# Token sums of a Strassen FFN made between the rows of the output projection, and two whole gate columns per FFN where there were four

## The chip, the cores and the metric

One core of one Trainium2 chip runs the whole kernel as one program. The metric is the device time of that program in microseconds, the median of several executions; lower is better. The core has five engines that each run their own stream of instructions in order: PE (TensorE, matmuls), DVE (VectorE), ACT (ScalarE), POOL (GpSimd) and SP (SyncE). SP and POOL issue the DMAs here. They wait for each other through semaphores.

## The reference

A two-layer decoder trunk over 512 tokens of width 1024, all in float32. Layer 0 mixes with a gated DeltaNet, layer 1 with sliding-window attention; both attend to 256 memory tokens as well. Each layer then adds the mixed heads through `w_out`, and a SwiGLU FFN of width 2816:

```python
x = x + jnp.concatenate([mix_out.astype(x.dtype), mem_o.astype(x.dtype)], axis=-1) @ w_out[layer]
x = x + swiglu(rms_norm(x, ln_ffn[layer]), w_gate_up[layer], w_down[layer])
...
def swiglu(h, w_gate_up, w_down):
    gu = h @ w_gate_up
    return (jax.nn.silu(gu[..., :D_FF]) * gu[..., D_FF:]) @ w_down
```

The change touches the first line's product and sum, and the product `h @ w_gate_up` of the second.

## The kernel before

**Layout.** Everything is kept with features on the 128 partitions and the 512 tokens along the free axis. The residual stream is eight tiles `x0` to `x7` (trace name `x`, 128 x 512), one for each block of 128 features.

**Exact products.** Float32 accuracy comes from splitting every operand into a high part and a remainder: ACT copies the high part (`whi` of a weight, `h` of an activation, line 148), DVE subtracts it from the original (`wlo` at L171, `l` at L171 or L174). A product of one 128 x 128 weight block is then three matmuls (`mm3`, L154): `whi` with `h`, `whi` with `l`, `wlo` with `h`. A *row* or *column* of 128 output features needs eight blocks, 24 matmuls of 512 tokens. A weight tile is loaded by SP into one of two `wraw` buffers (L197), split into one of three `whi`/`wlo` buffers, and its `wraw` buffer is free for the next load only when DVE has made `wlo`.

**Output rows.** `output` (both layers) makes eight rows of the output projection, row `m` for `x[m]`, `m` from 0 to 7. The three first rows are begun ahead, in pieces between the last steps of the mixer (`rest`), and end together; the others follow one by one. After a row DVE adds it into `x[m]`, ACT and DVE make the FFN's activation `h`, `l` from `x[m]` and its gain (`split_gain`), and the squares are added up (`sq`, `sqa`) for the norm. The norm's factor `rstd` is multiplied in after the FFN's products.

**Columns of the FFN.** The FFN has 22 gate and 22 up columns. Most are made two at a time by `quarters`, a Strassen-Winograd scheme: the two columns' weights and the tokens are cut in halves, and seven products with half the features and half the tokens take the place of eight. Each product is 12 matmuls of 256 tokens into a bank `g`, and needs one 512-wide weight tile (`wraw`, or a sum of two weight blocks `ws`, which SP loads and POOL adds to with an accumulating DMA) split by ACT and DVE. It also needs sums over the two halves of the tokens: `token_sums(j)` makes four of them from `x[j]` and `x[j+4]`: one small product (`fs`), four quarter-size instructions (`fu`), two copies on ACT and two subtractions on DVE into `T` tiles. All four sets, j = 0 to 3, must exist before the first product `t1`.

**What fills the time until then.** In the first half of each FFN (`f0 == 0`) gate columns 0 to 3 are made whole, 24 matmuls of 512 tokens each into banks `pj`; the norm's two matmuls stand inside column 1. The token sums are written behind columns 0 and 1 (j = 0, 1) and behind columns 2 and 3 (j = 2, 3). Then come the up columns 0 and 1 by quarters, and so on; ten pairs in this half.

**What sets the order.** Each engine runs its stream in order. The streams are put together by the framework's scheduler from the program order and a model of its own, so an instruction may stand earlier or later in its engine's stream than it was written. A tile pool's memory is given to a later pool when its scope has closed, and the first writer of the new tile waits for the last reader of the old.

## Time and profile before

| | |
|---|---|
| median of 3 executions | 1141.31 us (1141.19 to 1141.54) |
| the profiled execution | 1140.89 us |
| its span | 1139.0 us |
| mean granted TensorE clock | 0.998 |

The span is the time from the first to the last instruction of the trace; the execution's own time is 1.9 us longer. All stamps below are microseconds from the start of the span. The stages that matter here: layer 0's output rows run from about 255 to 305, its gate columns 0 to 3 until 327.8, the quarters until 427; layer 1's rows end at about 788.6, its gate columns at 810.9, its quarters at 910. In a row of a timeline stand start, length, engine, line, operation, output <- input, shape, count, and in brackets the engine's idle time before it and what ended that.

### The profile page before, as it was taken

How to read it: one execution, taken by the hardware profiler on the slowest of the kernel's cores; microseconds unless marked ns; L12 is line 12 of the kernel's file. 1: busy time of each engine (PE TensorE's matmuls, PEld its weight loads, DVE VectorE, ACT ScalarE, POOL GpSimd, SP SyncE). 2: the span in 40 equal slices, each digit the busy share in tenths (PEclk: the TensorE clock that was granted, in tenths of full speed). 3: DMA queues.
4: the chain of work that ended last, by engine and by line, in shares of the span. 5: the costliest groups of instructions: out<-in, count | busy, mean ns of one | idle time of the engine just before them, and what ended most of it. 6: DMA issues, size and time to landing. Idle time of an engine off the chain costs nothing.

```text
span 1139.0 us, 19670 instructions
## 1 busy us (share of the span) xinstructions
PE 1121.6 (98%) x7476; PEld 992.7 (87%) x7476; DVE 841.6 (74%) x1592; ACT 632.1 (55%) x1274; POOL 86.2 (8%) x97
## 2 busy tenths in 40 slices
PE   7999999999999999999999999999999999999996
PEld 6888887887899998899998888888999988999986
DVE  6754887776889987389876868959799743899754
ACT  7569572365566653256653656855566522566533
POOL 0120000000101100011100000010011100111000
PEclk9999999999999999999999999999999999999999
DMA  8434342324667744567723421153477733677232
GB/s 311 128 114 113 120 107 98 95 91 148 188 145 188 186 129 126 159 146 188 185 72 93 134 74 57 43 133 122 126 183 179 199 98 106 150 185 185 70 99 91
DMA packets 73971, 152.76 MB, mean 134 GB/s; under 512 B 17756, under 2 KB 18420, under 8 KB 73876
## 3 DMA queue, kind: packets, MB, share of 16 engines
q1 hardware_dynamic: 62356, 130.52, 37.4%
q0 software_dynamic: 11520, 20.98, 11.7%
q8 instruction: 59, 0.97, 0.4%
q14 instruction: 36, 0.29, 0.1%
HBM read 144.51 MB, written 6.96 MB: 133 GB/s over the span
## 4 chain that ended last, share of the span: by engine, by line
PE 95%; DVE 2%; ACT 1%; DMA 1%; issue 0%; SPq 0%; DVEq 0%; ACTq 0%
PE pj L154 47%; PE g L154 37%; PE sc L154 6%; PE pt L154 2%; PE qk L154 2%; PE pt L168 1%; PE g L168 1%; DMA wraw<-in_wmk 1%; DVE wlo L171 1%; ACT whi L148 0%; ACT sm L142 0%; SPq L329 0%; DVE x L171 0%; DVE l L174 0%; DVE stats L836 0%
## 5 line engine op out<-in xcount | busy, mean ns | idle before, releaser
L148 ACT ACTIVATE whi<-wraw 128x512 fp32r<-128x512 f32 (+2 forms) x331 | 244.1, 746 | 241.9 <-PE pj L154 151.2
L171 DVE TENSOR_TENSOR wlo<-wraw,whi 128x512 fp32r<-128x512 f32 (+2 forms) x331 | 273.0, 835 | 105.8 <-ACT whi L148 99.8
L154 PE MATMUL pj<-h,whi 128*128 128x512 f32 (+1 forms) x676 | 265.4, 393 | 0.1
L154 PE MATMUL pj<-l,whi 128*128 128x512 f32 (+1 forms) x676 | 263.7, 390 | 0.0
L154 PE MATMUL pj<-h,wlo 128*128 128x512 f32 (+1 forms) x676 | 263.4, 390 | 0.0
L154 PE MATMUL g<-T,whi 128*128 128x256 f32 x1280 | 228.1, 278 | 0.2
L154 PEld LDWEIGHTS g<-T,whi 128*128 128x128 f32 x1280 | 194.7, 188 | 1.8 <-DVE fu L174 1.8
L154 PE MATMUL g<-T,wlo 128*128 128x256 f32 x640 | 177.8, 278 | 0.0
L154 PEld LDWEIGHTS pj<-h,whi 128*128 128x128 f32 x676 | 126.9, 188 | 28.4 <-issue 3.5
L154 PEld LDWEIGHTS pj<-h,wlo 128*128 128x128 f32 x676 | 127.0, 188 | 25.8 <-DVE wlo L171 0.4
L154 PEld LDWEIGHTS pj<-l,whi 128*128 128x128 f32 x676 | 127.1, 188 | 24.7 <-DVE l L171 0.4
L154 PE MATMUL g<-h,whi 128*128 128x256 f32 (+1 forms) x492 | 138.4, 281 | 0.0
L154 PE MATMUL g<-h,wlo 128*128 128x256 f32 (+1 forms) x492 | 138.0, 280 | 0.0
L154 PE MATMUL g<-l,whi 128*128 128x256 f32 (+1 forms) x492 | 138.0, 280 | 0.0
L154 PEld LDWEIGHTS g<-T,wlo 128*128 128x128 f32 x640 | 120.1, 188 | 0.0
L154 PEld LDWEIGHTS g<-l,whi 128*128 128x128 f32 x492 | 92.3, 188 | 0.8 <-issue 0.2
L154 PEld LDWEIGHTS g<-h,whi 128*128 128x128 f32 x492 | 92.3, 188 | 0.8 <-issue 0.2
L154 PEld LDWEIGHTS g<-h,wlo 128*128 128x128 f32 x492 | 92.3, 188 | 0.5
L1104 POOL DMA_DIRECT2D ws<-in_wgu x40 | 35.3, 882 | 705.7 <-ACT sq L151 237.7
L148 ACT ACTIVATE whi<-ws 128x512 fp32r<-128x512 f32 x80 | 50.4, 631 | 49.3 <-PE g L154 40.2
L171 DVE TENSOR_TENSOR fu<-pj,rstd 128x512 f32<-128x512 f32 (+1 forms) x34 | 22.4, 660 | 54.3 <-PE pj L154 54.2
L171 DVE TENSOR_TENSOR wlo<-ws,whi 128x512 fp32r<-128x512 f32 x80 | 54.9, 686 | 6.4 <-ACT whi L148 6.3
(384 smaller groups left out, 1649.4 us busy)
## 6 DMA issues: line engine op xcount, KB each, us to landing
wraw<-in_wgu SPq DMA_DIRECT2D x48, 512.0 KB, 4.3
ws<-in_wgu SPq DMA_DIRECT2D x80, 256.0 KB, 3.6
ws<-in_wgu POOLq DMA_DIRECT2D x80, 256.0 KB, 4.9
wraw<-in_wdn SPq DMA_DIRECT2D x48, 384.0 KB, 3.2
wraw<-in_win SPq DMA_DIRECT2D x26, 512.0 KB, 3.6
wraw<-in_wgu SPq DMA_DIRECT2D x40, 256.0 KB, 4.7
wraw<-in_wout SPq DMA_DIRECT2D x16, 512.0 KB, 3.6
wraw<-in_wdn SPq DMA_DIRECT2D x16, 256.0 KB, 2.7
```

What stands on the lines that cost most here:

```text
L148: self.copied = self.nc.scalar.activation(out, in_, AF.Copy, **kw).ins
L154: return self.chained(self.nc.tensor.matmul(out, lhsT, rhs, start=start, stop=stop, skip_group_check=more).ins)
L168: return self.chained(self.nc.tensor.transpose(out, in_, self.ident[:k, :k]).ins)
L171: return eng.tensor_tensor(out=out, in0=a, in1=b, op=op).ins
L1104: nc.gpsimd.dma_start(s1, a22, accum_op=ALU.add)
```

## The change

It does three things.

1. The rows of the output projection are made in the order of `TURN`, 0 4 1 5 2 6 3 7. A row's place in the order is now called `r`; the bank goes by `r`, the weights, the gain and the `x` tile by `TURN[r]`. The gate columns take the blocks of `h` in the same order.
2. After every second row but the last, `output` makes the token sum of the two tiles just finished: j = 0, 1 and 2. The helper tiles come from the `sq` buffers (the small product) and a new pool `turn` (`raw`, two tiles); the six `T` tiles come from a new pool `tok` that stays open to the end. The fourth sum, j = 3, is made in the FFN.
3. Only gate columns 0 and 1 are whole. Gate columns 2 and 3 are made by `quarters` like the others.

At the end of the program the six `T` buffers of `tok` and the two of the FFN's pool serve where eight of the FFN's pool did.

```diff
+TURN = (0, 4, 1, 5, 2, 6, 3, 7)
...
+                    self.tok = pool("tok")
...
-        def part(m, *ks):
-            if m not in rows:
-                rows[m] = self.weight(self.a["wout"][layer, m]), self.row_bank(m), []
-            w, ps, done = rows[m]
+        def part(r, *ks):
+            if r not in rows:
+                rows[r] = self.weight(self.a["wout"][layer, TURN[r]]), self.row_bank(r), []
+            w, ps, done = rows[r]
...
+        def work():
+            return self.t(xp, [P, T], F32, "sq", 2)[:, :T // 2], [self.t(tp, [P, T], F32, "raw", 2) for _ in range(2)]
+
+        def row(r, *ks):
+            ps = part(r, *ks)
             if ps is None:
                 return
+            m = TURN[r]
             self.tt(nc.vector, self.x[m], ps, self.x[m], ALU.add)
-            hl = self.pair(hpool)
-            self.split_gain(self.x[m], self.gain(G_FFN[layer], m), *hl)
-            h.append(hl)
+            h[m] = self.pair(hpool)
+            self.split_gain(self.x[m], self.gain(G_FFN[layer], m), *h[m])
             self.acc = self.accumulate(xp, self.acc, self.x[m])
+            if r % 2 and r < KD - 1:
+                sums.append(self.token_sums(layer, r // 2, h, work, self.tok, 6))
...
-            return self.project(col(f, 0), h, "pj", between=between)
+            return self.project(col(f, 0), h, "pj", TURN, between=between)
+
+        def work():
+            return self.t(fp, [P, T // 2], F32, "fs", 3), [self.t(fp, [P, T], F32, "fu", 3) for _ in range(2)]
...
                 two = [gate(0), gate(1, {1: [norm]})]
                 whole += [gated(ps) for ps in two]
-                sums += [self.token_sums(fp, layer, f, h) for f in range(2)]
-                for f in (2, 3):
-                    whole.append(gated(gate(f)))
-                    sums.append(self.token_sums(fp, layer, f, h))
+                sums.append(self.token_sums(layer, 3, h, work, fp, 2))
```

**Layer 1, DVE, from the end of the first three rows.** Before, with the tile's own number in its name (`x0_` is tile x0, `wlo_1342` the fifth row's weight remainder, `wlo_1349` the sixth's):

```order
L171 TENSOR_TENSOR x0_546_2807<-pj_1282_7762,x0_546_2807 128x512
L171 TENSOR_TENSOR x1_547_2808<-pj_1301_7871,x1_547_2808 128x512
L171 TENSOR_TENSOR wlo_1335_8058<-wraw_1333_8055,whi_1334_8057 128x1024
L174 SCALAR_TENSOR_TENSOR l_1325_8028<-x0_546_2807,gains_2_67,h_1324_8027 128x512
L171 TENSOR_TENSOR x2_548_2809<-qk_1313_7935,x2_548_2809 128x512
L174 SCALAR_TENSOR_TENSOR l_1328_8038<-x1_547_2808,gains_2_67,h_1327_8037 128x512
L171 TENSOR_TENSOR sqa_1326_8031<-sqa_1326_8031,sq_1329_8041 128x512
L174 SCALAR_TENSOR_TENSOR l_1331_8049<-x2_548_2809,gains_2_67,h_1330_8048 128x512
L171 TENSOR_TENSOR sqa_1326_8031<-sqa_1326_8031,sq_1332_8052 128x512
L171 TENSOR_TENSOR wlo_1342_8097<-wraw_1340_8094,whi_1341_8096 128x1024
```

The same place after the change begins in the same way, with x0, x4, the fourth row's remainder, an `l`, x1 and an `l`. From there on (`wlo_1354` is the fifth row's remainder):

```order
L172 TENSOR_TENSOR sqa_1328_8102<-sqa_1328_8102,sq_1331_8112 128x512
L179 TENSOR_SCALAR sq_1332_8116<-x0_546_2807,gains_2_67 128x256
L175 SCALAR_TENSOR_TENSOR l_1338_8135<-x1_547_2808,gains_2_67,h_1337_8134 128x512
L175 SCALAR_TENSOR_TENSOR raw_1333_8117<-x0_546_2807,gains_2_67,sq_1332_8116 128x256
L175 SCALAR_TENSOR_TENSOR raw_1334_8118<-x4_550_2811,gains_2_67,sq_1332_8116 128x256
L175 SCALAR_TENSOR_TENSOR raw_1333_8117<-x4_550_2811,eps_5_71,raw_1333_8117 128x256
L172 TENSOR_TENSOR sqa_1328_8102<-sqa_1328_8102,sq_1339_8138 128x512
L175 SCALAR_TENSOR_TENSOR raw_1334_8118<-x4_550_2811,eps_5_71,raw_1333_8117 128x256
L172 TENSOR_TENSOR T_1336_8125<-raw_1333_8117,T_1335_8124 128x512
L172 TENSOR_TENSOR x5_551_2812<-pj_1343_8147,x5_551_2812 128x512
L172 TENSOR_TENSOR T_1336_8125<-raw_1334_8118,T_1335_8124 128x512
L172 TENSOR_TENSOR wlo_1354_8197<-wraw_1352_8194,whi_1353_8196 128x1024
```

The whole token sum of x0 and x4, and the add of the fourth row into x5, now stand ahead of the fifth row's remainder.

**Layer 0, DVE, the same place.** After the change x0, the fourth row's remainder, x1, an `l`, the fifth row's remainder, x4, the small product, an `l` and an `sqa` come first; then (`wlo_592` is the sixth row's remainder):

```order
L175 SCALAR_TENSOR_TENSOR raw_564_2873<-x0_546_2807,gains_2_67,sq_563_2872 128x256
L175 SCALAR_TENSOR_TENSOR raw_565_2874<-x4_550_2811,gains_2_67,sq_563_2872 128x256
L175 SCALAR_TENSOR_TENSOR raw_564_2873<-x4_550_2811,eps_5_71,raw_564_2873 128x256
L175 SCALAR_TENSOR_TENSOR l_569_2891<-x1_547_2808,gains_2_67,h_568_2890 128x512
L175 SCALAR_TENSOR_TENSOR raw_565_2874<-x4_550_2811,eps_5_71,raw_564_2873 128x256
L172 TENSOR_TENSOR T_567_2881<-raw_564_2873,T_566_2880 128x512
L172 TENSOR_TENSOR sqa_559_2858<-sqa_559_2858,sq_570_2894 128x512
L172 TENSOR_TENSOR x5_551_2812<-pj_574_2903,x5_551_2812 128x512
L172 TENSOR_TENSOR T_567_2881<-raw_565_2874,T_566_2880 128x512
L172 TENSOR_TENSOR wlo_592_2992<-wraw_590_2989,whi_591_2991 128x1024
```

Before, the sixth row's remainder stood directly behind the add of the fourth row, and the fifth row's remainder directly ahead of that add; no part of a token sum stood among the rows of layer 0 until the seventh was done.

**Layer 0, SP, the first loads of the FFN.** Before (1024-wide `wraw` are the whole gate columns 0, 1, 2 and 3; `ws_647` and `ws_648` are the first pair's weight sums):

```order
L197 DMA wraw_603_3083<-in_wgu 128x1024
L197 DMA wraw_607_3114<-in_wgu 128x1024
L197 DMA wraw_624_3186<-in_wgu 128x1024
L1102 DMA ws_647_3286<-in_wgu 128x512
L197 DMA wraw_634_3234<-in_wgu 128x1024
L1103 DMA ws_648_3287<-in_wgu 128x512
L1107 DMA wraw_649_3292<-in_wgu 128x512
```

After (gate columns 0 and 1, then the first pair's and the second pair's own columns, `wraw_636` and `wraw_654`, then the first pair's sums):

```order
L198 DMA wraw_618_3133<-in_wgu 128x1024
L198 DMA wraw_622_3164<-in_wgu 128x1024
L198 DMA wraw_636_3223<-in_wgu 128x1024
L198 DMA wraw_654_3341<-in_wgu 128x1024
L1110 DMA ws_637_3225<-in_wgu 128x512
L1111 DMA ws_638_3226<-in_wgu 128x512
L1115 DMA wraw_639_3231<-in_wgu 128x512
```

The first sum's load moved behind a fourth 1024-wide load, which waits for the remainder of gate column 1. In layer 1 the loads of the first two pairs' sums, issued between 738.8 and 754.8 before, moved behind the load of the first pair's own column, which waits for the remainder of gate column 0.

More of the change, by code (lines that the diff above doesn't have):

```diff
@@ L282, in rest @@
                                 row(m, k)
-                    h = self.output(xp, 0, part, self.bpool, rest)
+                    h, sums = self.output(xp, 0, part, self.bpool, rest)
             with opened("ffn0", side="right") as fp, self.banks(pj=2, g=6):
-                self.ffn(fp, xp, 0, h, self.apool, rope=True)
+                self.ffn(fp, xp, 0, h, sums, self.apool, rope=True)
             with self.banks(pj=2, qk=1, pt=4):
@@ L289, in build @@
                     mix, rest = self.swa(sp, xp)
-                    h = self.output(xp, 1, self.opened_rows(1, mix), self.apool, rest)
+                    h, sums = self.output(xp, 1, self.opened_rows(1, mix), self.apool, rest)
             with opened("ffn1", side="right") as fp, self.banks(pj=2, g=6):
-                self.ffn(fp, xp, 1, h, self.bpool)
+                self.ffn(fp, xp, 1, h, sums, self.bpool)
     def load_constants(self, cp):
@@ L903, in attend, with row_bank @@
         return steps
-    def row_bank(self, m):
-        if m % 3 < 2:
+    def row_bank(self, r):
+        if r % 3 < 2:
             return self.bank("pj")
@@ L932, in output, with ffn @@
         self.weng = nc.vector
-        h = []
+        h, sums = {}, []
         self.acc = None
-        def row(m, *ks):
-            ps = part(m, *ks)
+        def work():
+            return self.t(xp, [P, T], F32, "sq", 2)[:, :T // 2], [self.t(tp, [P, T], F32, "raw", 2) for _ in range(2)]
+        def row(r, *ks):
+            ps = part(r, *ks)
             if ps is None:
                 return
+            m = TURN[r]
             self.tt(nc.vector, self.x[m], ps, self.x[m], ALU.add)
-            hl = self.pair(hpool)
-            self.split_gain(self.x[m], self.gain(G_FFN[layer], m), *hl)
-            h.append(hl)
+            h[m] = self.pair(hpool)
+            self.split_gain(self.x[m], self.gain(G_FFN[layer], m), *h[m])
             self.acc = self.accumulate(xp, self.acc, self.x[m])
-        if ahead is not None:
-            ahead(row)
-        for m in range(len(h), KD):
-            row(m, 6, 7, 0, 1, 2, 3, 4, 5)
-        return h
-    def ffn(self, fp, xp, layer, h, apool, rope=False):
+            if r % 2 and r < KD - 1:
+                sums.append(self.token_sums(layer, r // 2, h, work, self.tok, 6))
+        with self.tc.tile_pool(name="turn", bufs=1, reuse_waits="tile") as tp:
+            if ahead is not None:
+                ahead(row)
+            for r in range(len(h), KD):
+                row(r, 6, 7, 0, 1, 2, 3, 4, 5)
+        return h, sums
+    def ffn(self, fp, xp, layer, h, sums, apool, rope=False):
         nc, a = self.nc, self.a
@@ L956, in ffn @@
         acc = self.acc
-        acts, sums, open_pairs, places = [], [], [], []
+        acts, open_pairs, places = [], [], []
         col = lambda f, up: a["wgu"][layer, 2 * f + up]
@@ L1045, in ffn @@
             parts = (slice(0, T // 2), slice(T // 2, T))
-            own = dict(pool=fp, tags=("T", "T"), bufs=8)
+            own = dict(pool=self.tok, tags=("T", "T"), bufs=6)
             w = {m: [down(m, j, n, **(own if m == KD - 1 else {})) for j, n in ((0, 6), (6, half - 6))] for m in range(tail, KD)}
-            outs = [[self.t(fp, [P, D], F32, "T", 8).rearrange("p (k t) -> p k t", k=4) for _ in range(2)] for t in parts]
+            outs = [[self.t(p, [P, D], F32, "T", n).rearrange("p (k t) -> p k t", k=4) for _ in range(2)]
+                    for p, n in ((self.tok, 6), (fp, 2))]
             for o, t in zip(outs, parts):
@@ L1067, in ffn, with token_sums @@
                 self.store(ps, r, o, t, tail)
-    def token_sums(self, fp, layer, j, h):
+    def token_sums(self, layer, j, h, work, pool, bufs):
         q = T // 2
@@ L1078, in token_sums @@
         x0, x1 = self.x[j], self.x[j + 4]
-        c = self.t(fp, [P, q], F32, "fs", 3)
-        raw = [self.t(fp, [P, T], F32, "fu", 3) for _ in range(2)]
+        c, raw = work()
         t = [x[:, i * q:(i + 1) * q] for x in raw for i in range(2)]
@@ L1086, in token_sums @@
         self.stt(t[3], x1[:, :q], n1, t[1], ALU.mult, ALU.subtract)
-        hl = [self.t(fp, [P, D], F32R, "T", 8) for _ in range(2)]
+        hl = [self.t(pool, [P, D], F32R, "T", bufs) for _ in range(2)]
         for x, i in zip(raw, (0, T)):
```

## The prediction

> **What bounds the kernel now.** I read the page's shares and its chain first, then the chain in order of time around the two FFNs, then each engine's timeline where the chain leaves PE. The page's busy shares and chain shares, and rows of the chain in order of time (start, length, what, number of records):

> ```profile
> PE 1121.6 (98%) x7476; PEld 992.7 (87%) x7476; DVE 841.6 (74%) x1592; ACT 632.1 (55%) x1274; POOL 86.2 (8%) x97
> ```
> ```profile
> PE 95%; DVE 2%; ACT 1%; DMA 1%; issue 0%; SPq 0%; DVEq 0%; ACTq 0%
> ```
> ```profile
> 294.72 17.68 PE pj L154 x78
> 312.86 14.98 PE pj L154 x66
> 327.84 96.60 PE g L154 x828
> 424.44 1.14 PE pj L154 x5
> 425.58 1.64 PE g L154 x12
> ```

> PE's own stream sets the end; in these rows each piece follows the last (0.46 at 312.4 is the norm's two matmuls), and it runs so through the columns, the quarters and into the down projections. So two things count: how much PE work goes, and whether PE now waits. Prices: a 512-wide matmul takes 17.68/78 = 0.227 us, so a row or a whole column (24 of them) 5.44. The ten pairs of columns made by quarters (7 products of 12 matmuls, 840 in all) take 96.60 + 1.64 = 98.2 us: 0.117 each, 1.40 a product, 9.82 a pair.

> **What goes.** Per FFN two whole columns leave (2 x 5.44 = 10.88) and one pair by quarters comes (9.82): 1.06 us saved, **2.1 us** in both. All of it is on the path. No token sum's arithmetic is added or removed: 1 + 4 + 2 instructions on DVE and 2 on ACT per sum, as before. But they move from under the gate columns to between the rows, and there each row's first use of its weight remainder (wlo, made by DVE) can wait behind them.

> **Layer 1, the fourth and fifth rows.** The first three rows end together. DVE's timeline of before from there, three rows of it further on for the parts of a sum, then ACT's and PE's:

> ```profile
> 759.39 1.37 DVE L171 TENSOR_TENSOR x<-pj,x 128x512 f32<-128x512 f32 x2 [0.93 <-PE pj L154]
> 760.67 1.22 DVE L171 TENSOR_TENSOR wlo<-wraw,whi 128x1024 fp32r<-128x1024 f32 x1
> 761.82 0.75 DVE L174 SCALAR_TENSOR_TENSOR l<-x,gains,h 128x512 fp32r<-128x512 f32 x1
> 762.48 0.69 DVE L171 TENSOR_TENSOR x<-qk,x 128x512 f32<-128x512 f32 x1
> 763.08 0.74 DVE L174 SCALAR_TENSOR_TENSOR l<-x,gains,h 128x512 fp32r<-128x512 f32 x1
> 763.74 0.69 DVE L171 TENSOR_TENSOR sqa<-sqa,sq 128x512 f32<-128x512 f32 x1
> ...
> 765.61 1.22 DVE L171 TENSOR_TENSOR wlo<-wraw,whi 128x1024 fp32r<-128x1024 f32 x1
> ```
> ```profile
> 769.09 0.61 DVE L178 TENSOR_SCALAR fs<-x,gains 128x256 f32<-128x256 f32 x2
> 769.62 0.48 DVE L174 SCALAR_TENSOR_TENSOR fu<-x,gains,fs 128x256 f32<-128x256 f32 x1
> 770.01 0.75 DVE L174 SCALAR_TENSOR_TENSOR l<-x,gains,h 128x512 fp32r<-128x512 f32 x1
> ```
> ```profile
> 766.25 1.06 ACT L148 ACTIVATE whi<-wraw 128x1024 fp32r<-128x1024 f32 x1 [1.69 <-DMA wraw<-in_wout]
> ```
> ```profile
> 761.95 0.50 PE L154 MATMUL pj<-h,wlo 128*128 128x512 f32 x1
> ...
> 766.85 0.63 PE L154 MATMUL pj<-h,wlo 128*128 128x512 f32 x2
> ```

> Start to start, DVE needs 0.60 for an x, sqa or T of 512, 0.66 for an l, 1.15 for a wlo of 1024, 0.26 for the small product and 0.39 for a quarter of a sum. Before, the fifth row's wlo came at 765.61 and ended at 766.83; PE started the fourth row's last matmul at 766.85 and went straight on, 0.23 later. After the change the same two rows of x start at 759.39 and the fourth row's wlo ends where it did, but the order puts fourteen instructions between it and the fifth row's wlo, where there were six: l, x, l, sqa, small product, l, three quarters, sqa, quarter, T, x, T. Their sum is 3 x 0.66 + 2 x 0.60 + 2 x 0.60 + 0.26 + 4 x 0.39 + 2 x 0.60 = 7.4. From 761.82 that is 769.2, and the wlo ends at 770.4. The first T also waits for ACT's copy, queued behind a whi that started at 766.25 when its load landed: with that the copy ends at 767.9 (1.06 and a copy's 0.6 later), T, x and T at 769.7 and the wlo at 770.9. PE has two matmuls of the sixth row to do from 767.08 (0.45), then nothing until the wlo: **a hole of 2.9 to 3.4 us**, plus 0.1 for the restart (the second matmul at 761.95 came 0.33 after the first, not 0.23). I take 3.3, towards the row of ACT as it stands. The later rows of layer 1 have cover: the sixth row's wlo follows an l, an sqa and a small product later and ends at about 773.6, against a fifth row that ends at 775.9 (22 matmuls after 770.9). DVE stays ahead from there.

> **Layer 0, the same place.** Rows of DVE's, ACT's and PE's timelines of before, and the landing of two loads of x:

> ```profile
> 277.17 1.22 DVE L171 TENSOR_TENSOR wlo<-wraw,whi 128x1024 fp32r<-128x1024 f32 x1 [0.18 <-ACT whi L148]
> ```
> ```profile
> 284.56 1.06 ACT L148 ACTIVATE whi<-wraw 128x1024 fp32r<-128x1024 f32 x1 [3.03 <-DMA wraw<-in_wout]
> ```
> ```profile
> 283.48 0.39 PE L154 MATMUL pj<-h,wlo 128*128 128x512 f32 x1
> 283.97 0.50 PE L154 MATMUL pj<-mq0h,wlo 128*128 128x512 f32 x1
> ```
> ```profile
> L276 SPq DMA_DIRECT2D x<-in_xT x2: 375/402/430, 274.6 to 275.0; - x2
> DMA to landing us min/median/max: 6.7/6.8/6.9
> ```

> The order puts the fifth row's wlo early here (ahead of the third x add), so before's own hole goes: 283.48 is the fourth row's last matmul and 283.97 the next, a hole of 0.26 and a restart of 0.1. What is late next is the sixth row's wlo. The second row is now tile x4, whose load, issued at 274.6, lands at 281.3; DVE would reach its add at 280.7 (wlo, x, l, wlo from 277.17). From 281.35 come x, small product, l (waiting for ACT's h until 282.8), sqa, three quarters, l, quarter: 286.3. The first T needs ACT's copy, again behind the whi that starts at 284.56: T at 286.7. Then T, sqa, x, T make 289.1, and the wlo ends at 290.3. PE, without its old hole, ends the fifth row at 288.7, does two matmuls each of the sixth and seventh rows until 289.6 and waits 0.7. From one wlo to the next DVE then needs l, sqa, small product, x, three quarters, l, quarter, sqa and the wlo: 6.1, while PE has 24 matmuls, 5.4: a second hole of 0.6. Two restarts make 1.5; less 0.36, layer 0's rows cost **1.2 us**. Bounds: with neither load late DVE would end the sixth row's wlo at 288.7, no hole, and the gain is 0.36; with each 1 us later, a loss of about 2.2.

> **The first quarters in layer 0.** The pair's loads are now needed 11 us sooner, and SP's queue puts the second pair's whole column ahead of them, which waits for gate column 1's wlo. Of before, SP's two issues that follow such a wlo, POOL's second add, the landing times of POOL's first add (issued at 302.83) and of this second, and ACT's steps from the norm on, with two copies that follow each other:

> ```profile
> 302.36 0.33 SPq L197 DMA_DIRECT2D wraw<-in_wgu  x1
> 302.74 0.42 SPq L1103 DMA_DIRECT2D ws<-in_wgu  x1
> ```
> ```profile
> 307.55 0.87 POOL L1105 DMA_DIRECT2D ws<-in_wgu  x1 [3.60 <-ACT h L148]
> ```
> ```profile
> DMA to landing us min/median/max: 7.2/7.2/7.2
> ```
> ```profile
> DMA to landing us min/median/max: 5.3/5.3/5.3
> ```
> ```profile
> 312.89 0.69 ACT L142 ACTIVATE rstd<-g,eps 128x512 f32<-128x512 f32 x1 [0.31 <-PE g L154]
> 313.61 0.63 ACT L142 ACTIVATE rstd<-rstd 128x512 f32<-128x512 f32 x1
> 314.26 1.28 ACT L133 ACT_TABLE_LOAD   x1
> ```
> ```profile
> 319.46 0.63 ACT L148 ACTIVATE whi<-wraw 128x512 fp32r<-128x512 f32 x1 [0.61 <-DMA wraw<-in_wgu]
> 320.00 0.61 ACT L148 ACTIVATE whi<-ws 128x512 fp32r<-128x512 f32 x1
> ```

> Laid on as above, that wlo ends at 305.7 (the whole column was issued at 302.36 before). The load follows 0.4 later, POOL's add 4.8 after it as at 302.74 to 307.55, so 310.9, and it lands 5.3 later, as the add at 307.55 did: 316.2. From that landing ACT has five copies or whi (2.65), Ln, Exp and table (2.65), a silu and the fifth product's whi (1.15), DVE its wlo (0.69): 7.1, so 323.3. PE started the quarters at 327.84; two columns less and 1.2 of holes more make 318.2, and it reaches the fifth product 5.6 later, 323.8. It just fits: 0, and 1.4 if the add takes the 7.2 us of the first add of before. In layer 1 the same loads leave at about 783 for a start of the quarters near 803: covered.

> **The sum.** -2.1 + 3.3 + 1.2 + 0 = **+2.4 us**. The profiled execution took 1140.89 us (span 1139.0), 0.42 under the median 1141.31; on the median the forecast is **1143.7**. A measurement tells about 0.2% of this kernel from no change, 2.3 us: below 1139.0 is faster, above 1143.6 slower, and the forecast lies on that edge.

> **Rivals.** (a) *The rows stay covered.* If DVE keeps ahead in both layers, the saving stands alone: -2.1 to -2.5, 1138.8 to 1139.2. For it: over the span DVE is busy only 74%. Against it: 7.4 us of DVE work stand in one piece where PE has 24 matmuls, 5.4. Half a failure (layer 1's hole only) gives 1142.2. (b) *The add is late* in layer 0: PE waits 1.4 ahead of the fifth product, 1145.1. It decides from a landing later than 316.7. For it: before's first add took 7.2 us; against: that one went out at the head of the burst of loads, this one late in it, like the second. (c) *The pause lowers PE's clock.* If the clock fell to half for as long as the 3.3 us pause, PE would lose 1.7: 1145.4. Against it is the windows view, in which the first 4 us hold no matmul and the granted clock is 1.00 (stretch, its length, busy time and count of PE, PEld, DVE, ACT and POOL, granted clock, DMA share, GB/s):

> ```profile
> 0.00:4.00 4.00, 0.00 (x0) 0.00 (x0) 0.56 (x5) 1.28 (x1) 0.52 (x5) 1.00 0.37 93
> ```

> [...] (d) *The change doesn't do what it says*: the instruction order has 36 more matmuls per FFN, 84 for 48, so this is out but for trouble elsewhere.

> **How the numbers follow.** Forecast with both layers' holes 0.5, (a) with its half failure 0.2, (b) 0.18, (c) 0.07, others 0.05. The forecast's own range, from the bounds 2.9 to 3.5, -0.4 to 2.2 and 0, is +0.4 to +3.6: 1141.7 to 1144.9. With (b) and half of (a) the range is 1140.4 to 1146.2. Slower takes half of the forecast's chance and all of (b) and (c), 0.5; faster a part of (a), 0.08; within 0.2% the rest, 0.42.

> **What would show it.** In layer 1 a hole of about 3 us in PE ahead of the fifth row's third matmul, with DVE's T and x adds before the wlo; in layer 0 two holes under 1 us ahead of the sixth and seventh rows; 9.8 us for the eleventh pair by quarters; none or little ahead of the first pair's fifth product. No hole in layer 1 proves the main step wrong; a hole at the first quarters proves (b).

## The result, and the profile after

The changed kernel takes **1150.56 us** (median of 5 executions, 1147.55 to 1151.54), the kernel before 1141.24 (1140.86 to 1141.54): a ratio of **1.008**, 95% interval 1.007 to 1.0091. It is slower by 9.3 us. The forecast was 1143.7 and the range ended at 1146.2, so the sign was right and the size was not. The profiled execution is the one of 1150.56 us; its span is 1148.8, 9.8 longer than before. In kernel.py of the changed kernel most line numbers are one higher (matmuls L155, copies L149, subtractions L172).

The page's busy times and its chain shares, as shown of before:

```profile
PE 1123.5 (98%) x7548; PEld 997.3 (87%) x7548; DVE 851.3 (74%) x1614; ACT 638.8 (56%) x1290; POOL 90.2 (8%) x101
```
```profile
PE 87%; DVE 7%; ACT 2%; DMA 2%; issue 1%; SPq 0%; DVEq 0%; ACTq 0%
```

PE was busy 1121.6 us before and is busy 1123.5 us now, although 2.5 us of its work went. And the chain leaves PE: its share there falls by 8 points, 5 of which DVE takes. Where, the chain in order of time shows (start, length, what, number of records):

```profile
324.82 105.42 PE g L155 x888
...
776.21 6.89 PE pj L155 x22
783.11 4.99 PE qk L155 x22
788.09 17.68 PE pj L155 x78
```

Before, the chain was on PE from 283.97 on in layer 0, the fifth row. Now it comes onto PE for good only at 324.82 there, inside the first quarters, and at 776.21 in layer 1, at the fifth row. Of the rows of layer 1 the first 22 matmuls take 6.89 us, the next 22 take 4.99: after the pause PE is not only late but slow. PE's timeline has the waits themselves (idle time and its end in brackets):

```profile
296.39 0.50 PE L155 MATMUL pj<-mq0h,wlo 128*128 128x512 f32 x1 [0.39 <-DVE wlo L172]
...
324.82 0.51 PE L155 MATMUL g<-T,whi 128*128 128x256 f32 x2 [3.98 <-ACT fs L149]
...
776.21 0.69 PE L155 MATMUL pj<-h,wlo 128*128 128x512 f32 x1 [2.87 <-DVE wlo L172]
```

And the windows view, in stretches of 3.41 us laid around these pauses (stretch, length, busy time and count of PE, PEld, DVE, ACT and POOL, granted clock, DMA share, GB/s):

```profile
322.39:325.80 3.41, 0.98 (x8) 0.98 (x9) 2.53 (x4) 3.17 (x8) 0.66 (x1) 1.00 0.48 79
325.80:329.21 3.41, 3.41 (x18) 3.41 (x18) 1.44 (x3) 0.91 (x2) 0.00 (x0) 0.50 0.86 307
...
772.95:776.36 3.41, 0.54 (x3) 0.15 (x2) 3.41 (x6) 1.87 (x3) 0.00 (x0) 1.00 0.02 5
776.36:779.77 3.41, 3.41 (x9) 2.63 (x10) 3.41 (x7) 0.00 (x0) 0.00 (x0) 0.50 0.51 154
```

Behind each pause the granted clock is 0.50 for 3.41 us: 1.7 us of PE's work are lost each time. Measured from one named row of PE's timeline to the next, the 9.8 us divide as follows:

| stage (from, to) | before | after | difference |
|---|---|---|---|
| start to `sc<-N,ones`: the mixer and the rows' first pieces | 266.57 | 267.27 | +0.70 |
| to layer 0's norm (`g<-sq,ones`): its rows | 45.66 | 46.04 | +0.38 |
| to its first down projection (`ac11h`): columns, quarters | 121.19 | 125.76 | +4.57 |
| to layer 1's norm: attention and its rows | 361.83 | 366.54 | +4.71 |
| to layer 1's first `ac11h`: columns, quarters | 121.22 | 119.96 | -1.26 |
| to the last row of PE (`g<-fg,ones`) | 213.96 | 214.03 | +0.07 |
| to the end of the span (output) | 8.57 | 9.20 | +0.63 |

Layer 1's columns and quarters are undisturbed, so **1.26 us** is what the two columns less save in an FFN. With the same saving in layer 0, its +4.57 is -1.26 + 3.98 of pause + 1.7 of clock, and 0.15 left over; layer 1's rows are 2.87 + 1.7 and 0.14 left over. What is left over is of the size of a restart: behind the first pause the two matmuls from 324.82 to 325.16 take 0.34 us, where two take 0.23. The first line can't be put down to the change: in the profiles of the kernels below, which have the changed rows too, this stretch ended between 266.35 and 267.51. The last was 8.6 to 9.2 in them; it was not looked into.

### The profile page after: what moved, and what is told of

It is laid out like the page before. It is cut to its first block, busy times and chain, and to the rows that moved or that the text cites. A ratio compares the mean times of both kernels' runs of the same rounds, so it can differ in the third digit from the quotient of the medians.

```text
span 1148.8 us, 19876 instructions
## 1 busy us (share of the span) xinstructions
PE 1123.5 (98%) x7548; PEld 997.3 (87%) x7548; DVE 851.3 (74%) x1614; ACT 638.8 (56%) x1290; POOL 90.2 (8%) x101
## 4 chain that ended last, share of the span: by engine, by line
PE 87%; DVE 7%; ACT 2%; DMA 2%; issue 1%; SPq 0%; DVEq 0%; ACTq 0%
PE pj L155 39%; PE g L155 38%; PE sc L155 6%; DVE wlo L172 2%; PE pt L155 2%; PE qk L155 1%; PE pt L169 1%; DMA wraw<-in_wgu 1%; DVE btmp L172 1%; DVE big L172 1%; ACT whi L149 1%; DMA wraw<-in_wmk 1%; ACT sm L143 1%; PE g L169 1%; DVE x L172 0%
## 5 line engine op out<-in xcount | busy, mean ns | idle before, releaser
L149 ACT ACTIVATE whi<-wraw 128x512 fp32r<-128x512 f32 (+2 forms) x337 | 246.0, 739 | 234.9 <-PE pj L155 137.6
L172 DVE TENSOR_TENSOR wlo<-wraw,whi 128x512 fp32r<-128x512 f32 (+2 forms) x337 | 274.8, 825 | 102.8 <-ACT whi L149 96.6
L155 PE MATMUL pj<-h,wlo 128*128 128x512 f32 (+1 forms) x644 | 251.6, 391 | 2.9 <-DVE wlo L172 2.9
L155 PE MATMUL pj<-h,whi 128*128 128x512 f32 (+1 forms) x644 | 254.2, 395 | 0.1
L155 PE MATMUL pj<-l,whi 128*128 128x512 f32 (+1 forms) x644 | 251.8, 391 | 0.0
L155 PE MATMUL g<-T,whi 128*128 128x256 f32 x1344 | 240.0, 278 | 4.1 <-ACT fs L149 4.0
L155 PEld LDWEIGHTS g<-T,whi 128*128 128x128 f32 x1344 | 204.6, 188 | 5.7 <-ACT fs L149 4.2
L155 PE MATMUL g<-T,wlo 128*128 128x256 f32 x672 | 186.9, 278 | 0.0
L155 PEld LDWEIGHTS pj<-h,wlo 128*128 128x128 f32 x644 | 121.3, 188 | 28.1 <-DVE wlo L172 3.7
L155 PE MATMUL g<-h,whi 128*128 128x256 f32 (+1 forms) x516 | 145.6, 282 | 0.0
L155 PE MATMUL g<-l,whi 128*128 128x256 f32 (+1 forms) x516 | 145.2, 281 | 0.0
L155 PE MATMUL g<-h,wlo 128*128 128x256 f32 (+1 forms) x516 | 145.1, 281 | 0.0
L155 PEld LDWEIGHTS pj<-h,whi 128*128 128x128 f32 x644 | 121.3, 188 | 27.2 <-issue 3.5
L155 PEld LDWEIGHTS pj<-l,whi 128*128 128x128 f32 x644 | 121.5, 189 | 23.7 <-DVE l L172 0.4
L155 PEld LDWEIGHTS g<-T,wlo 128*128 128x128 f32 x672 | 126.3, 188 | 0.0
L155 PEld LDWEIGHTS g<-h,whi 128*128 128x128 f32 x516 | 97.4, 189 | 0.8 <-issue 0.2
L155 PEld LDWEIGHTS g<-l,whi 128*128 128x128 f32 x516 | 97.4, 189 | 0.8 <-issue 0.2
L155 PEld LDWEIGHTS g<-h,wlo 128*128 128x128 f32 x516 | 97.4, 189 | 0.5
L149 ACT ACTIVATE whi<-ws 128x512 fp32r<-128x512 f32 x84 | 53.0, 631 | 55.5 <-PE g L155 43.3
L172 DVE TENSOR_TENSOR wlo<-ws,whi 128x512 fp32r<-128x512 f32 x84 | 57.6, 685 | 7.4 <-ACT whi L149 7.3
L172 DVE TENSOR_TENSOR fu<-pj,rstd 128x512 f32<-128x512 f32 (+1 forms) x34 | 22.4, 659 | 52.7 <-PE pj L155 52.7
```

The source lines that it names most:

```text
L149: self.copied = self.nc.scalar.activation(out, in_, AF.Copy, **kw).ins
L155: return self.chained(self.nc.tensor.matmul(out, lhsT, rhs, start=start, stop=stop, skip_group_check=more).ins)
L172: return eng.tensor_tensor(out=out, in0=a, in1=b, op=op).ins
```

## The experiments

All but one (pauses) were built from the changed kernel. The kernel before ran beside them on the same chip, with medians of 1140.7 to 1141.0; the ratios are against it.

**1. The loads of the first quarters, earlier (ws_first).** On SP's queue two 1024-wide loads, the first and the second pair's own columns, are held behind the loads of the first stacked halves (`ws`). The edit acts in both layers:

```diff
-        a1 = self.load(src[0])
+        raw = self.t(self.wpool, [P, D], F32, "wraw", 2)
+        a1, first = raw, nc.sync.dma_start(raw, src[0]).ins
...
+        if len(self.held_back) == 1:
+            self.nosync(first, ws)
```

> The four loads of stacked halves for layer 0's first pair by quarters (ws) go out ahead of the two whole columns that wait for buffers; nothing else is moved on purpose. Theory A (the pause of 3.98 us at the first quarters comes from these loads: POOL's add landed at 316.3, ACT's table chain and the held copies were queued behind it): the add lands some 5 us sooner, the pause goes, and the 3.4 us at granted clock 0.50 that follow it go too: 1150.6 - 4.1 - 1.7 = 1144.8 (1144 to 1146), layer 1's pause stays. Rival B (ACT's own queue is too long, wherever the loads are): a pause of 3 us or more stays there, 1149 to 1151.

Measured: 1145.39 us (1145.32 to 1147.27), 1.0042 [1.0029, 1.0055], in the range of A. POOL's adds went out at 305, not 312 to 313. PE's row at the place of the pause:

```profile
322.26 0.50 PE L155 MATMUL g<-T,whi 128*128 128x256 f32 x2 [1.64 <-ACT fs L149]
```

The pause is shorter by 2.34 us, but not gone, and the clock stays 1.00 behind it. Rival B's pause of 3 us or more did not come, yet ACT is still late by 1.64. Its rows show a second copy ahead of the norm, of weights that DVE had still to add up:

```profile
316.05 0.63 ACT L149 ACTIVATE whi<-wraw 128x512 fp32r<-128x512 f32 x1 [1.29 <-DVE wraw L172]
316.58 0.67 ACT L143 ACTIVATE rstd<-g,eps 128x512 f32<-128x512 f32 x1
```

**2. The norm first on ACT, the loads left late (norm_first).** In `quarters`, for the first pair of either layer:

```diff
             self.split(raw, *w)
+            if lead:
+                self.nosync(self.copied, self.table_ins)
```

> The changed kernel with one thing moved: on ACT the copies (whi) for layer 0's first pair by quarters stand behind the norm's Ln, Exp and table load, not ahead of them; the loads stay as late as they are. Theory A (the pause of 3.98 us at the first quarters is the queue: the first whi waits for the load that lands at 316.3, and the norm's chain of 2.7 us, two silus and the held copy that PE waits for stand behind it): Ln starts at about 313.9, the table is there by 316.4, the held copy is done by 320 to 321, the pause falls to 0.3 to 0.8 us with no drop of the clock: 1150.6 - 3.5 - 1.7 = 1145.4 (1144.5 to 1147). Rival B (the late load alone makes it): a pause of 3 us or more stays.

Measured: 1145.51 us (1143.42 to 1146.25), 1.0037 [1.0025, 1.005]. First ACT's rows of the changed kernel at that place, then those of this one:

```profile
316.33 0.63 ACT L149 ACTIVATE whi<-ws 128x512 fp32r<-128x512 f32 x1 [4.32 <-DMA ws<-in_wgu]
...
319.03 0.67 ACT L143 ACTIVATE rstd<-g,eps 128x512 f32<-128x512 f32 x1
...
320.39 1.28 ACT L134 ACT_TABLE_LOAD   x1
321.79 0.63 ACT L143 ACTIVATE fg<-fg 128x512 f32<-128x512 f32 x1
...
324.40 0.36 ACT L149 ACTIVATE fs<-g 128x256 f32<-128x256 f32 x1
```
```profile
313.43 0.69 ACT L143 ACTIVATE rstd<-g,eps 128x512 f32<-128x512 f32 x1 [0.95 <-PE g L155]
...
314.81 1.28 ACT L134 ACT_TABLE_LOAD   x1
316.10 0.63 ACT L143 ACTIVATE fg<-fg 128x512 f32<-128x512 f32 x1
...
320.01 0.37 ACT L149 ACTIVATE fs<-g 128x256 f32<-128x256 f32 x1
```

In the changed kernel ACT stands idle for 4.32 us at a copy whose load lands at 316.3; the norm's first step behind it had been ready since the norm's matmuls on PE, 313.31 to 313.93. Moved ahead, it starts at 313.43, and the held copy (`fs`) starts at 320.01, not at 324.40, though the loads are as late as ever. PE's timeline has no pause over 0.3 us there. So the pause is made by the **order of ACT's queue around a late load**; mending either end takes most of it away. The gain has a price, seen in both layers:

```profile
317.53 0.28 PE L155 MATMUL g<-l,whi 128*128 128x256 f32 x1
317.83 0.51 PE L155 MATMUL g<-T,whi 128*128 128x256 f32 x2
318.17 0.28 PE L155 MATMUL g<-h,wlo 128*128 128x256 f32 x1
```

The scheduler now puts two matmuls of the second product (`g<-T,whi`) into the first, and so twice more. From `g<-l` to `g<-h` pass 0.64 us for three matmuls that take 0.35.

**3. The rows' half alone (rows_only).** Four whole columns again:

```diff
                 sums.append(self.token_sums(layer, 3, h, work, fp, 2))
+                for f in (2, 3):
+                    whole.append(gated(gate(f)))
```

> Only the rows' half of the change: order 0 4 1 5 2 6 3 7, three sums between rows, the fourth in the FFN, but four whole columns per FFN as before (no PE work is saved). Theory A: the first quarters start 11 us later, so their loads and the norm are done in time, and layer 0 has no pause there; layer 1's pause of about 2.9 us and its clock drop of 1.8 us stay: 1141.0 + 0.4 + 4.7 = 1146 (1145 to 1147). Rival B (the pause at the quarters comes from the sums' place and not from the two columns less): 1150 or more.

Measured: 1145.85 us (1144.38 to 1146.69), 1.0042 [1.003, 1.0055]. Layer 0 from the norm to the down projections takes 121.22 us, before 121.19, with no pause; layer 1 has its own:

```profile
770.71 0.50 PE L155 MATMUL pj<-h,wlo 128*128 128x512 f32 x1 [2.81 <-DVE wlo L172]
```

A holds: the pause at the first quarters is the price of the two columns less, the pause in layer 1 that of the sums' place.

**4. Layer 1's sums later (late1).** In `output`, for layer 1:

```diff
+            if layer and 4 <= r < KD - 1:
+                sums.append(self.token_sums(layer, r - 4, h, work, self.tok, 6))
             m = TURN[r]
...
-            if r % 2 and r < KD - 1:
+            if not layer and r % 2 and r < KD - 1:
```

> In layer 1 alone the three token sums come three rows later in the program (sum 0 behind the fifth row's weights, and so on), so the fifth row's wlo stands ahead of sum 0 on DVE; layer 0 is as in the changed kernel. Theory A (seven us of DVE work ahead of that wlo make the pause of 2.87 us, and the clock's drop behind it costs 1.8 more): the pause goes, 1150.6 - 4.7 = 1145.9 (1145 to 1147). Rival B (DVE has too little time between rows wherever the sums are): holes of 0.5 to 1 us turn up ahead of later rows, 1147 to 1149.

Measured: 1146.82 us (1145.81 to 1147.98), 1.0052 [1.004, 1.0064], A's size. DVE's remainder of the fifth row in the changed kernel (the last of these rows), and in this one (`x2`: the fifth's and the sixth's), with PE's one wait left in layer 1:

```profile
766.36 1.22 DVE L172 TENSOR_TENSOR wlo<-wraw,whi 128x1024 fp32r<-128x1024 f32 x1
...
774.35 0.68 DVE L172 TENSOR_TENSOR T<-raw,T 128x512 fp32r<-128x512 f32 x1
774.95 1.21 DVE L172 TENSOR_TENSOR wlo<-wraw,whi 128x1024 fp32r<-128x1024 f32 x1
```
```profile
770.20 2.36 DVE L172 TENSOR_TENSOR wlo<-wraw,whi 128x1024 fp32r<-128x1024 f32 x2
```
```profile
794.17 0.50 PE L155 MATMUL pj<-h,wlo 128*128 128x512 f32 x1 [0.52 <-DVE wlo L172]
```

Rival B's hole turns up too, but once and small: gate column 0's remainder is now 0.52 late.

**5. The sums later in both layers (late_sums).** As 4, without `layer and`.

> The sums come later in both layers. With that the scheduler also puts layer 0's first ws loads ahead of the whole columns on SP's queue. Theory A: both pauses and both drops of the clock go, the saving of 2.1 us on PE's stream stands alone but for holes under 0.5 us: 1139 to 1141, at or below the kernel before (1141.2). Rival B (something else than the pauses costs time in the changed kernel): 1143 or more.

Measured: 1147.2 us (1144.31 to 1149.38), 1.005 [1.0038, 1.0062]: a miss for A. Layer 1 is as in run 4. In layer 0 ACT's and PE's rows say why:

```profile
314.31 0.63 ACT L149 ACTIVATE whi<-ws 128x512 fp32r<-128x512 f32 x1 [2.86 <-DMA ws<-in_wgu]
...
319.15 0.63 ACT L149 ACTIVATE whi<-wraw 128x512 fp32r<-128x512 f32 x1 [1.56 <-DVE wraw L172]
```
```profile
324.64 0.50 PE L155 MATMUL g<-T,whi 128*128 128x256 f32 x2 [2.77 <-ACT fs L149]
```

SP's queue was better, but the whole columns' loads came later with the later rows, so POOL's adds moved from 311.8 only to 307.9, and ACT again stood idle at that copy, ahead of the norm. A second copy, of weights that DVE had still to add up, even stood between the norm's two steps and waited 1.56 us more. A pause of 2.77 us stayed, and with it the clock's drop (0.50 from 325.44 to 328.85); the rows of layer 0 had a hole of 0.86 as well. The two kinds of pause are not one: each needs its own repair.

**6. The pauses filled with matmuls that nobody reads (filled).**

```diff
+    def fill(self, ps, w, x, n):
+        self.lock(True)
+        self.latest = self.last
+        for _ in range(n):
+            self.mm(ps, w, x, True, True)
...
+        if lead:
+            self.fill(pb, w[0][:, :P], sums[0]["t1"][0], 30)
...
```

> The changed kernel with matmuls added that nobody reads: 30 of 256 columns ahead of the first pair's third product in layer 0 (3.5 us of the pause of 3.98) and 11 of 512 ahead of the fifth row's third matmul in layer 1 (2.5 us of the pause of 2.87). The wait for the data is untouched. Theory A (a pause of TensorE drops its clock to half for 3.4 us afterwards): granted clock 1.00 behind both places, and although 41 matmuls are added the time falls by 1.7 + 1.8 = 3.5 us to 1147 (1146.5 to 1148). Rival B (the slow matmuls behind the pauses have another cause, such as the weights' loads): the clock still drops, 1150 to 1151.

Measured: 1147.69 us (1146.71 to 1148.83), 1.0058 [1.0046, 1.007]: 2.9 us less than the changed kernel, with 41 matmuls more. The windows behind the two places:

```profile
322.00:326.00 4.00, 3.03 (x26) 2.83 (x25) 3.11 (x6) 3.88 (x8) 0.86 (x1) 1.00 0.17 39
326.00:330.00 4.00, 3.95 (x33) 3.95 (x34) 3.17 (x6) 2.33 (x5) 0.00 (x0) 1.00 1.01 302
...
776.00:780.00 4.00, 3.67 (x17) 2.99 (x17) 4.00 (x8) 0.00 (x0) 0.00 (x0) 1.00 0.44 131
```

The wait for the data is no shorter (the added matmuls end 1.02 and 0.33 us before it does), yet the clock is 1.00. So here it is PE's idleness that drops the clock. By the medians the two drops cost about 3 us of the 9.3, by the two windows 3.4.

**7. Which pauses drop the clock (pauses).** The kernel before, with a chain of DVE work and an unread matmul between rows of the down projections:

```diff
+                if m:
+                    d = self.t(fp, [P, T // 2], F32R, "fs", 3)
+                    for i in range(m + 1):
+                        self.tt(nc.vector, d, self.x[m - 1][:, :T // 2], (d if i else self.x[m - 1][:, :T // 2]).bitcast(F32), ALU.max)
+                    self.mm(ps[:, :T // 2], self.onesr, d, True, True)
```

> The kernel before with added work: between the rows of the down projections TensorE's order is fixed and a matmul that nobody reads waits for one to eight extra operations of DVE on the row just ended, so TensorE pauses about 30 times for 1.5 to 5 us (the time as such tells nothing). The question is which pauses drop the granted clock. Theory A (the clock is set for a window of 3.41 us on a fixed grid, and is half where TensorE was active in less than half of the window before): no drop behind a pause under 1.7 us, always one behind 3.4 us or more, and between them it depends on how the pause lies on the grid; the starts of all drops lie a whole number of 3.41 us apart. Rival B (a pause of itself drops it once it is longer than some limit between 1.64 and 2.77 us): the length alone decides, and the drops begin at the same distance behind each pause's start.

Measured: 26 pauses, of 3.27 to 7.43 us, each with a drop (longer than meant, so it says nothing on shorter ones). Two of them in PE's timeline, and the windows view around each, laid on the edges of the drops:

```profile
1027.30 0.58 PE L154 MATMUL pj<-fs,ones 128*128 128x256 f32 x1 [3.27 <-DVE fs L171]
...
1251.22 0.39 PE L154 MATMUL pj<-fs,ones 128*128 128x256 f32 x1 [4.21 <-DVE fs L171]
```
```profile
1023.14:1026.55 3.41, 0.89 (x4) 0.39 (x3) 2.44 (x4) 0.84 (x1) 0.00 (x0) 1.00 0.25 94
1026.55:1029.96 3.41, 2.66 (x7) 2.18 (x8) 0.66 (x2) 0.00 (x0) 0.00 (x0) 0.50 0.40 115
1029.96:1033.38 3.42, 3.42 (x10) 2.65 (x9) 0.00 (x0) 0.00 (x0) 0.00 (x0) 0.50 0.00 0
```
```profile
1245.00:1248.41 3.41, 2.02 (x9) 1.32 (x8) 1.86 (x3) 0.84 (x1) 0.00 (x0) 1.00 0.28 77
1248.41:1251.83 3.42, 0.61 (x3) 0.56 (x4) 2.69 (x6) 0.63 (x1) 0.00 (x0) 1.00 0.40 115
1251.83:1255.24 3.41, 3.41 (x10) 2.65 (x9) 0.00 (x0) 0.00 (x0) 0.00 (x0) 0.50 0.00 0
```

The shorter pause costs two stretches at half clock, the longer one only one. All edges of the clock inside this span (found with the windows view in stretches of 0.1 us) lie to within 0.02 us on one grid, of 3.413 us: the first drop is at 436.04, the last at 1323.51, 887.47 us or 260.0 times 3.413 later. From a pause's start to its drop pass 2.0 to 5.2 us. So A's grid holds, and rival B's fixed distance falls. Its limit of length was not put to the test here.

**8. Repairs together (best, best2, best4).** All start from run 4's layer 1. *best* has repairs 1 and 2 as they are; *best2* has repair 1, holds only the third product's copies behind the table load, in layer 0 only, and moves layer 1's third sum on into the FFN; *best4* has run 4's layer 1 unchanged, repair 1 in layer 0 only, the third product's copies behind the table load there, and

```diff
         p1 = held(pa)
+        if lead:
+            self.nosync(self.silus[1], self.copied)
```

> All three repairs at once: norm first on ACT, the ws loads ahead on SP's queue (both for layer 0's first pair), sums three rows later in layer 1. Theory A: no pause over 0.6 us is left in either place and the granted clock stays 1.00 up to the end of the stream; the saving of 2.1 us less 0.5 to 1.2 us of small holes: 1139.2 to 1140.2, that is 0.9992 to 0.9984 of the kernel before measured beside it. Rival B (as with the sums later in both layers, another wait takes the place): 1142 or more.

> As the run with all three repairs, with three differences: on ACT only the third product's copies stand behind the table load, and in layer 0 only, so that TensorE's order of products is not mixed (there, three times per FFN, two matmuls of the next product ran ahead, each for 0.3 us lost, 0.9 per layer); and in layer 1 the third sum moves on into the FFN, behind gate column 0's weights, whose wlo was 0.45 us late. Theory A: no pause over 0.4 us in the two places, granted clock 1.00, quarters as fast as in the changed kernel (120.0 us from the norm to the down projections, against 121.2 before): 1141.0 - 2.1 + 0.3 = 1139.2 (1138.8 to 1140.2), below the kernel before. Rival B: the held copy is late again (a pause of 0.5 to 1.6 us at the first quarters): 1140 to 1141.5.

> The last try at a version that keeps the saving: layer 1 exactly as in the run with the late sums there alone; in layer 0 the loads early, only the third product's copies behind the table load, and the second silu behind the held copy that TensorE waits for. Theory A: layer 1's stages take 0.1 us less than before (as there), layer 0's pause at the first quarters shrinks to 0.5 us or less with the order of products kept, so layer 0 gains 0 to 0.5 us: 1140.4 to 1141.6, not told from the kernel before. Rival B (the held copy is late all the same, by the silu that waits for DVE): 0.8 us more there, up to 1142.5.

Measured: *best* 1142.44 us (1142.03 to 1144.13), 1.0017 [1.0008, 1.0026]; *best2* 1143.73 (1143.14 to 1146.39), 1.0027 [1.0016, 1.0038]; *best4* **1141.39** (1140.46 to 1142.64), **1.0004 [0.9994, 1.0013]**. *best* and *best2* lie above what theory A gave them. *best* has no pause over 0.5 us and no drop in the two places, but the mixing of run 2 takes some 0.9 us in each layer (120.95 and 120.90 us from the norm to the down projections, against 119.96). *best2* got rid of the mixing and gave new waits on ACT, the second in layer 1, behind the sum that was moved there:

```profile
321.98 0.51 PE L155 MATMUL g<-T,whi 128*128 128x256 f32 x2 [0.79 <-ACT fs L149]
...
807.29 0.51 PE L155 MATMUL g<-T,whi 128*128 128x256 f32 x2 [1.81 <-ACT fs L149]
```
```profile
804.30:807.71 3.41, 1.60 (x14) 1.40 (x13) 2.58 (x5) 3.09 (x8) 0.86 (x1) 1.00 0.25 55
807.71:811.12 3.41, 3.41 (x18) 3.41 (x17) 2.67 (x4) 1.75 (x5) 0.00 (x0) 0.50 0.97 284
```

Here a pause of only 1.81 us, which lies whole in one stretch, halved the clock for the next.

*best4* came out as theory A had it, 9.2 us under the changed kernel. It is not told from the kernel before. Its stages from `sc<-N,ones` to the first down projections take 166.29 us in layer 0 against 166.85, and from layer 0's to layer 1's 482.89 against 483.05: 0.7 us of the 2.5 saved are left, and holes of 0.17 to 0.46 us (the longest at 789.20, gate column 0 of layer 1) and their restarts take nearly all of the rest back. No version that was run is faster than the kernel before.

## Why the prediction was wrong, step by step

- **The saving, -2.1.** Right in kind; it is -2.5 (1.26 an FFN).
- **Layer 1's fifth row, +3.3.** Right. The fourteen instructions took from 767.50 to 774.95 on DVE, 7.45 us where 7.4 was worked out, and PE waited 2.87, just under the bound of 2.9 to 3.4; with 0.14 left over that is 3.0. Run 4 removes it by moving the sum.
- **Layer 0's rows, +1.2.** Too much: +0.38, one hole of 0.39 at the seventh row. The sixth row's remainder came when it was to come (290.23 against 290.3), but PE got there 0.7 later, as its stream ran 0.7 later, while x4, issued 0.7 later too, landed at 281.2 instead of 281.3. In run 1, which started at 266.56, the holes are 0.31 and 0.37.
- **The first quarters, 0: the step that failed.** The landing was right (316.3, forecast 316.2). The path behind it was not: I laid ACT's chain against the fifth product, which PE reaches 5.6 us into the quarters. PE stopped at the third, 2.8 us in. The lines of `quarters`:

```python
        product(pa, a1[:, :T], "11", True)
        p1 = held(pa)
        product(pc, s1, "t1", True)
        p5 = held(pc)
        ...
        product(pa, a1[:, :T], "t2", False)
```

  The third product adds onto the bank of the first, so it must wait until ACT has copied that bank (`held`, the tile `fs`). I followed the products' weights and forgot this copy, which stands on ACT behind the norm's chain, two silus and three more copies. It ended at 324.76; PE was there at 320.84: 3.98 us, not 0. Rival (b) named the place and the late load, but its 1.4 came from the same wrong consumer. Runs 1, 2 and 3 show the cause from three sides.
- **Rival (c), the clock, given 0.07.** It happened behind both pauses, 3.4 us in all. Its 1.7 was my estimate, from half speed for as long as the pause; measured, the clock was 0.50 for 3.41 us behind the pause of 3.98 and behind the one of 2.87 alike. What I held against it, a granted clock of 1.00 in the first 4 us, is a stretch before any matmul, and the figure of 1.00 does not hold at the start. PE's first matmuls of the kernel before begin at 6.76; in its timeline matmuls of 256 columns start 0.21 us apart up to 10.6, as they do at a granted clock of 0.50 behind the first pause (326.76 and 326.97), and 0.12 from 10.8 on, while the windows view prints 1.00 throughout:

```profile
9.37 0.41 PE L154 MATMUL pj<-ml,whi 128*128 128x256 f32 x1
9.58 0.41 PE L154 MATMUL pj<-mh,wlo 128*128 128x256 f32 x1
...
11.04 0.28 PE L154 MATMUL pj<-ml,whi 128*128 128x256 f32 x1
11.15 0.28 PE L154 MATMUL pj<-mh,wlo 128*128 128x256 f32 x1
```
```profile
8.00:10.00 2.00, 2.00 (x11) 2.00 (x10) 1.62 (x4) 1.18 (x4) 0.00 (x0) 1.00 0.94 308
```

  So the trace that I had showed half speed behind idleness, in the spacing of the matmuls. At the pause of 3.3 us that I forecast myself, the price belonged in the sum.
- **The rest.** In sum: -2.5, +0.4, +4.1, +3.0, +3.4, and outside of the steps +0.7 at the start and +0.7 from the last rows to the end: 9.8. The spread of the five executions (1147.55 to 1151.54) is left open. A drop that comes or stays away by the grid's phase would give steps of 1.7 us, and the fastest one has the highest mean clock (0.996 against 0.993 and 0.994), but only one execution has a trace.

## What to carry to other kernels

When a phase is pulled forward, list for each step of the engine that bounds the kernel *all* that it waits for, the release of its output bank by another engine's copy as well as its inputs, and take the earliest step that can be late. Look for what stands ready behind an instruction that waits for a DMA: in the changed kernel the norm's chain stood ready on ACT for 5 us (313.93 to 319.03) behind one copy that waited 4.32 for its load. Check a clock figure against the spacing of the matmuls: in the kernel before those of 256 columns start 0.21 us apart up to 10.6 and 0.12 from 10.8 on, under a printed 1.00 throughout. And a pause of TensorE of some 2.8 us (five of five in these profiles dropped the clock to 0.50, and so did one of 1.81) is to be priced at 1.7 us more than its length, half of the 3.41 us that a drop lasted behind the two pauses of the changed kernel, or TensorE kept busy; a saving of 1.26 us per FFN doesn't pay for one such pause.
